# A hybrid diffusion backbone on one core: where the rounded half of a split operand is written

## The chip, the core and the metric

The kernel runs on one core of one Trainium2 chip. Its engines are TensorE (matrix products, into PSUM), VectorE (elementwise), ScalarE (copies and activation functions), GpSimd (elementwise, SBUF only) and SyncE, which here issues most of the DMAs. The metric is the device time of one execution in microseconds, the median of several runs.

## What is computed

Two layers over 1024 latent tokens of width 1024. Layer 0 mixes with pooling and differential attention, layer 1 with a gating MLP; each layer ends in an MLP with a squared ReLU. All data are float32. What matters here are three products of the same kind, each the second one of an MLP:

```python
def spatial_gating(h, w_in, ln_g, ln_b, sg_w, sg_b, w_out):
    ...
    return (u * mixed.reshape(b_, n, SG_WIDTH)) @ w_out      # (1024 x 2048) @ (2048 x 1024)

def sq_relu_ffn(h, w1, w2):
    return jnp.square(jax.nn.relu(h @ w1)) @ w2              # (1024 x 4096) @ (4096 x 1024)

for l in range(DEPTH):
    ...
    x = x + g1 * y                                           # l == 1: y = spatial_gating(...)
    x = x + g2 * sq_relu_ffn(modulate(...), ffn_w1[l], ffn_w2[l])
```

## The kernel before

Float32 accuracy is had from TensorE's rounded float32 type (F32R) by splitting each operand into a rounded half `hi` and the rest `lo` = x - hi. `split` (L101 to L104) does that with a ScalarE copy into `hi` (the write rounds) and a VectorE subtraction of `hi` from the source. `mm3` (L117 to L122) then makes three matmuls of each pair of operands: hi x hi (L120), hi x lo (L121), lo x hi (L122).

`ffn2` (L1239) is the second product of an MLP: layer 0's MLP, the gating MLP (weights `od_w_out`) and layer 1's MLP, in that order of time. The hidden values lie in DRAM (`hid_d`). Of the contraction, 512 rows at each end are done plainly (`accum`). What is between is done in blocks of 1024 rows: 3, 1 and 3 blocks. A block takes 7 products in place of 8 (Strassen's scheme in Winograd's form); each product has 4 token tiles of 128, and each tile 4 x 3 matmuls of 128x128 by 512 columns into one PSUM bank.

`block_prep` (L1122) is a generator that makes a block's operands. It loads the eight quarters of the block (`load`, L1127): four of hidden values (a11 to a22) and four of weights (b11 to b22), 1 MB each, and multiplies each weight quarter by the gate row on VectorE (L1137, both operands in SBUF). For each product `put` (L1152) splits the weights' operand in two halves of 128x1024 (`put_b`, L1140) and the hidden operand in four tiles of 128x512 (`put_a`, L1146). Between the products the quarters are added and subtracted in place, 128x2048 at a time, 8 a block, by GpSimd (L1169, L1172), but for two on VectorE in the first block of each second product (`E`, L1182). A quarter's buffer is loaded anew when its last reader is through.

`block` (L1209) runs the products. After each token tile VectorE adds the bank to U (L1229) or to the running result X (L1231); in a block's first product of a second product ScalarE copies it to U (L1227). Most banks are then accumulated on by the next product, so TensorE needs the add of that tile to be done before the next product's same tile. After each tile `step` takes one step of `block_prep`, four of which make the operands of one product. In layer 0's MLP every third step also makes one of 24 steps of layer 1's modulation (`ada_gen`, L141 to L169): 2 DMAs of 512 KB, 8 matmuls (L159) into a "tr" bank that is held over 8 such steps.

The order: TensorE and GpSimd keep the order of the program in `ffn2` (`pinned`, `pe_pool`). On the other engines and on SyncE's DMA queue a planner orders the instructions by its own costs, and each queue is then strictly in order. Buffers that hold work ahead: 8 tiles "hid" (one per token tile of a hidden operand, both halves), 10 tiles "w" (4 per weight operand), 8 tiles "h" for the quarters. PSUM has 8 banks: 5 "mm" for the products and 3 "tr" (`tr`, L92), used for transposes in other parts of the program and, in the blocks, by the modulation alone.

Of the kernel before, what the change touches and what calls it, by code (L numbers as in the profile page):

```python
# [10 lines left out]
F32R = mybir.dt.float32r  # L11
# [6 lines left out]
P = 128  # L18
# [12 lines left out]
SGW = 2048  # L31


# Issue order of the opening. The digit is a token tile (x, s, v, t, T, n), a block of 128 features
# (l, a, b, g, h, m), a pair of such blocks (w) or a piece of the rope tables (r).
# x/s/v/t/T/U: load, sum of squares, scale, transpose a token tile; l/a/b: load, multiply, turn the modulation into
# columns; g/h: modulate and split the first or second half of the tokens; w: weights of the first head;
# m/n: products of the first half by block or, for the last two blocks, by tile; q/r: rope tables; y: context tiles.
OPENING = (
# [7 lines left out]
class Net:  # L47
# [53 lines left out]
    def split(self, hi, lo, src):  # L101
        nc = self.nc
        nc.scalar.copy(out=hi, in_=src)  # L103
        nc.vector.tensor_sub(lo, src, hi.bitcast(F32))  # L104

    def load_split(self, src, shape, scale=None, mk=None):
        nc = self.nc
        mk = mk or self.w_tile
        raw = self.stage(shape)
        nc.sync.dma_start(out=raw, in_=src)  # L110
        if scale is not None:
            nc.vector.tensor_mul(raw, raw, scale)
        hi, lo = mk(shape), mk(shape)
        self.split(hi, lo, raw)
        return hi, lo
# [1006 lines left out]
    def block_prep(self, W, g2b, hp, n):  # L1122
        nc = self.nc
        G = nc.gpsimd
        raw, ahead = {}, {}

        def load(role, f0):  # L1127
            i, j = int(role[1]) - 1, int(role[2]) - 1
            t = self.big(self.h1 if role in ("b11", "a11", "b21", "a12") else self.h0, [P, 4, 512], F32)
            if role[0] == "a":  # L1130
                q = f0 // 256 + 2 * j
                for g in range(2):
                    nc.sync.dma_start(out=t[:, 2 * g:2 * g + 2], in_=self.hid_d[q + g, :, :, i * 512:(i + 1) * 512])
            else:
                s = slice(j * 512, (j + 1) * 512)
                nc.sync.dma_start(out=t, in_=W[f0 + i * 512:f0 + (i + 1) * 512, s].rearrange("(k p) n -> p k n", p=P))
                nc.vector.tensor_mul(t, t, g2b[:, s].unsqueeze(1).broadcast_to([P, 4, 512]))  # L1137
            ahead[role] = t

        def put_b(op, src, g, mk=None):  # L1140
            sh = [P, 2, 512]
            hi, lo = (mk or self.w_tile)(sh), (mk or self.w_tile)(sh)
            self.split(hi, lo, src[:, 2 * g:2 * g + 2])
            op[1].append((hi, lo))

        def put_a(op, src, ts):  # L1146
            for t in ts:
                z = hp.tile([P, 2, 4, P], F32R, tag="hid", name=self.name("hid"))
                self.split(z[:, 0], z[:, 1], src[:, :, t * P:(t + 1) * P])
                op[0].append(z)  # L1150

        def put(a, b, before=(), after=(), mk=None):  # L1152
            op = ([], [])
            self.ops.append(op)
            put_b(op, raw[b], 0, mk)
            yield
            put_b(op, raw[b], 1, mk)
            for f in before:
                f()
            yield  # L1160
            put_a(op, raw[a], (0, 1))
            yield
            put_a(op, raw[a], (2, 3))
            for f in after:
                f()
            yield

        def sub(o, x, y, eng=G):
            return lambda: eng.tensor_sub(raw[o], raw[x], raw[y])  # L1169

        def add(o, x, y, eng=G):
            return lambda: eng.tensor_add(raw[o], raw[x], raw[y])  # L1172

        for role in ("b11", "a11", "b21", "a12", "b22", "b12", "a21", "a22"):
            load(role, 512)
        for b in range(n):
            raw.update(ahead)
            f0 = 512 + (b + 1) * 1024
            more = b + 1 < n
            nx = lambda *roles: [lambda r=r: load(r, f0) for r in roles] if more else []  # L1180
            mk = None
            E = G if b else nc.vector  # L1182
            yield from put("a11", "b11", [sub("b12", "b22", "b12", E)], [sub("a11", "a11", "a21", E)])
            yield from put("a12", "b21", [add("b11", "b11", "b12"), sub("b21", "b21", "b11")])
            yield from put("a11", "b12", [sub("b12", "b22", "b11")], [add("a21", "a21", "a22")])
            yield from put("a22", "b21", nx("b11"), [sub("a22", "a22", "a11")] + nx("a11"))
            yield from put("a22", "b11", nx("b21"), [sub("a12", "a12", "a22")] + nx("b22"))
            yield from put("a21", "b12", nx("b12"), nx("a21"))
            if not more:
                halves = []  # L1190

                def mk(shape):
                    if not halves:
                        z = self.big(self.h1, [P, 4, 512])
                        halves.extend((z[:, 0:2], z[:, 2:4]))
                    return halves.pop(0)
            yield from put("a12", "b22", nx("a22"), nx("a12"), mk=mk)
# [255 lines left out]


class FfnPair:
    """One pair of feature tiles of the first product of an MLP: squared ReLU of it."""

    def __init__(self, net, i):
        self.net, self.i = net, i
# [17 lines left out]


class SgPair:
    """One group of the gating MLP: the gate times the values mixed along the tokens of a chunk."""  # L1480

    def __init__(self, net, i):
        self.net, self.i, self.v = net, i, {}
# [85 lines left out]
```

## Time and profile before

| | before |
|---|---|
| time, median of 3 runs | 2774.7 us (2770.87 to 2779.99) |
| span of the profiled execution | 2777.1 us |
| TensorE, matmul busy | 2612.3 us, 94% |
| VectorE busy | 1916.1 us, 69% |
| ScalarE busy | 1032.1 us, 37% |
| GpSimd busy | 993.7 us, 36% |

The page gives the span of the profiled execution, from its first to its last instruction, and no other time of it. In the rows PE is TensorE, DVE VectorE, ACT ScalarE, POOL GpSimd, SPq SyncE's DMA queue; L104 is line 104 of the kernel. An operation is written out<-in by the names of the program's tiles: `hid` is a split hidden tile, `w` a split half of weights, `h` a quarter, `ps` a product's bank, `x` the running result, `u` the tile U, `ad` the modulation's weights. A window has the stretch, its length, the busy time and number of instructions of PE, PEld (weight loads of TensorE), DVE, ACT and POOL, the granted TensorE clock as a share of full speed, the share of time that the DMA engines were busy, and GB/s. "[3.72 <-DVE x L1231]" says that the engine was idle for 3.72 us before, and that the DVE instruction of L1231 ended it. The end of a matmul is modelled, so its pace is read from the starts. A wait for several releasers is put down to the last.

### The profile page before, as it was taken

To read this page: it belongs to the slowest core of one execution; us is meant where nothing else is said; L and a number is where in the kernel's file an instruction comes from. 1 tells how busy PE (TensorE), PEld (TensorE's weight loads), DVE (VectorE), ACT (ScalarE), POOL (GpSimd) and SP (SyncE) were. 2 spreads that over 40 slices of the span, in tenths; PEclk is the share of its full clock that TensorE was granted. 3 is DMA by queue.
4 is the path that set the end of the run, shared out by engine and by line. 5 is a ranking of instruction groups with operands and counts; after the bars stand their busy time and mean duration, and the time that the engine had idled before them with its cause. 6 is when DMAs were issued, how large, how long until landed. Compare 5 with 4: busy or idle time off the path is not lost. (4 is left out here: it accounts for less than half of the span.)

```text
span 2777.1 us, 33164 instructions
## 1 busy us (share of the span) xinstructions
PE 2612.3 (94%) x12531; PEld 2128.2 (77%) x12531; DVE 1916.1 (69%) x2506; ACT 1032.1 (37%) x1827; POOL 993.7 (36%) x567
## 2 busy tenths in 40 slices
PE   6999989998999999979999999999899999988989
PEld 5888967777877888756677888887687888767767
DVE  5645678888486556698887624665978555689994
ACT  5322356666243333223334224542333333323330
POOL 5421357664053232144354202210545223043352
PEclk9999999999999999999999999999899999999999
DMA  8576532211233334544533323446032333622302
GB/s 259 169 220 212 194 112 97 91 63 41 97 110 103 121 107 135 211 166 171 205 106 133 117 93 110 136 152 238 24 122 77 121 106 121 241 92 91 121 8 91
DMA packets 202845, 360.15 MB, mean 130 GB/s; under 512 B 13231, under 2 KB 107266, under 8 KB 197566
## 3 DMA queue, kind: packets, MB, share of 16 engines
q1 hardware_dynamic: 183168, 290.01, 31.7%
q10 hardware_dynamic: 16158, 46.01, 4.5%
q0 software_dynamic: 3360, 22.02, 2.3%
q8 instruction: 99, 1.62, 0.2%
q14 instruction: 60, 0.49, 0.1%
HBM read 264.89 MB, written 93.10 MB: 129 GB/s over the span
## 5 line engine op out<-in xcount | busy, mean ns | idle before, releaser
L104 DVE TENSOR_TENSOR w<-s,w 128x512 fp32r<-128x512 f32 (+3 forms) x311 | 299.0, 976 | 208.8 <-ACT w L103 206.1
L120 PE MATMUL ps<-w,hid 128*128 128x512 f32 x928 | 378.6, 408 | 42.0 <-DVE x L1231 35.5
L122 PE MATMUL ps<-w,hid 128*128 128x512 f32 x928 | 371.7, 401 | 12.9 <-DVE hid L104 12.9
L121 PE MATMUL ps<-w,hid 128*128 128x512 f32 x928 | 371.6, 400 | 0.0
L103 ACT CAST w<-s 128x512 fp32r<-128x512 f32 (+2 forms) x313 | 212.6, 692 | 274.7 <-POOL s L1035 74.3
L1169 POOL TENSOR_TENSOR h<-h,h 128x2048 f32<-128x2048 f32 x36 | 176.1, 4892 | 256.5 <-DVE hid L104 91.9
L120 PEld LDWEIGHTS ps<-w,hid 128*128 128x128 f32 x928 | 180.7, 195 | 107.9 <-DVE x L1231 32.2
L103 ACT CAST hid<-h 128x512 fp32r<-128x512 f32 x196 | 116.6, 619 | 355.9 <-PE ps L122 184.6
L104 DVE TENSOR_TENSOR hid<-h,hid 128x512 fp32r<-128x512 f32 x196 | 234.9, 1213 | 8.8 <-ACT hid L103 8.7
L122 PEld LDWEIGHTS ps<-w,hid 128*128 128x128 f32 x928 | 180.6, 195 | 56.0 <-DVE hid L104 16.8
L121 PEld LDWEIGHTS ps<-w,hid 128*128 128x128 f32 x928 | 181.2, 195 | 36.8
L1035 POOL TENSOR_TENSOR s<-s,s 128x512 f32<-128x512 f32 x36 | 48.2, 1339 | 434.5 <-DVE w L104 434.3
L104 DVE TENSOR_TENSOR w<-h,w 128x1024 fp32r<-128x1024 f32 x92 | 184.8, 2013 | 2.3 <-ACT w L103 2.3
L1172 POOL TENSOR_TENSOR h<-h,h 128x2048 f32<-128x2048 f32 x14 | 77.2, 5513 | 272.3 <-DVE h L1169 185.7
L781 ACT ACTIVATE e<-sc,nm 128x1280 f32<-128x1280 f32 x96 | 127.5, 1328 | 108.3 <-DVE nm L775 106.6
L120 PE MATMUL ps<-h,w 128*128 128x512 f32 x416 | 164.0, 394 | 0.3 <-ACT h L205 0.3
L121 PE MATMUL ps<-h,w 128*128 128x512 f32 x416 | 162.3, 390 | 0.4 <-DVE h L206 0.4
L122 PE MATMUL ps<-h,w 128*128 128x512 f32 x416 | 162.6, 391 | 0.0
L765 PE MATMUL sc<-k,q 128*128 128x512 f32 (+1 forms) x576 | 139.1, 377 | 15.5 <-ACT e L781 14.0
L771 DVE TENSOR_REDUCE nm<-sc 128x1 f32<-128x768 f32 x192 | 148.5, 815 | 0.6 <-PE sc L765 0.6
L794 POOL TENSOR_TENSOR e<-e,e 128x1280 f32<-128x1280 f32 x47 | 136.4, 2902 | 3.9
L765 PEld LDWEIGHTS sc<-k,q 128*128 128x128 f32 x576 | 103.0, 192 | 42.2 <-ACT e L781 21.9
(313 smaller groups left out, 6405.7 us busy)
## 6 DMA issues: line engine op xcount, KB each, us to landing
ad<-in_ada_w_dram SPq DMA_DIRECT2D x96, 512.0 KB
s<-in_ffn_w_dram SPq DMA_DIRECT2D x80, 512.0 KB
hid_d<-h SPq DMA_DIRECT2D x28, 1024.0 KB
h<-hid_d SPq DMA_DIRECT2D x56, 512.0 KB
h<-in_ffn_w_dram SPq DMA_DIRECT2D x24, 1024.0 KB
s<-in_od_w_in_dram SPq DMA_DIRECT2D x32, 512.0 KB
k<-kt_d POOLq DMA_DIRECT2D x12, 1280.0 KB, 7.7
kt_d<-x SPq DMA_DIRECT2D x48, 256.0 KB
```

Source lines behind the costliest of these rows:

```text
L103: nc.scalar.copy(out=hi, in_=src)
L104: nc.vector.tensor_sub(lo, src, hi.bitcast(F32))
L120: nc.tensor.matmul(ps, ah, bh, start=first, stop=False, skip_group_check=more)
L121: nc.tensor.matmul(ps, ah, bl, start=False, stop=False, skip_group_check=more)
L122: nc.tensor.matmul(ps, al, bh, start=False, stop=last, skip_group_check=more)
L765: nc.tensor.matmul(s[:, o0:o0 + n], hd["q"][:, c, t * P:(t + 1) * P], hd["k"][:, c, a, o0:o0 + n], start=(a == 0), stop=(a == 1))
L771: self.nc.vector.tensor_reduce(st["nm"][c][:, i:i + 1], st["s"][c][:, s], axis=AX.X, op=ALU.max, negate=True)
L781: nc.scalar.activation(e, st["s"][c], AF.Exp, bias=nm[:, 0:1], accum_out=z)
L794: nc.gpsimd.tensor_add(e0, e0, e1)
L1035: G.tensor_add(a22, a21, a22)
L1169: return lambda: eng.tensor_sub(raw[o], raw[x], raw[y])
L1172: return lambda: eng.tensor_add(raw[o], raw[x], raw[y])
```

## The change

In `put_b` and `put_a`, and nowhere else, `split` is replaced by a new function `split_ps`. For each piece of 128x512 (a tile of `put_a` is one piece, a half of `put_b` two) ScalarE writes the rounded value to a "tr" PSUM bank as well, and VectorE subtracts that copy, not the one in SBUF. After the pieces, ScalarE writes the rounded half to SBUF, as before, for TensorE. So a tile of `put_a` takes two ScalarE copies of 128x512 and one subtraction; a half of `put_b` takes two copies of 128x512, two subtractions of 128x512 and a copy of 128x1024. The rest of the diff empties some comment lines.

```diff
+    def split_ps(self, hi, lo, src, parts):
+
+        nc = self.nc
+        for h, l, x in parts(hi, lo, src):
+            r = self.tr([P, 512]).rearrange("p (a n) -> p a n", a=x.shape[1])
+            nc.scalar.copy(out=r.bitcast(F32R), in_=x)
+            nc.vector.tensor_sub(l, x, r)
+        nc.scalar.copy(out=hi, in_=src)
...
         def put_b(op, src, g, mk=None):
             sh = [P, 2, 512]
             hi, lo = (mk or self.w_tile)(sh), (mk or self.w_tile)(sh)
-            self.split(hi, lo, src[:, 2 * g:2 * g + 2])
+            self.split_ps(hi, lo, src[:, 2 * g:2 * g + 2], lambda h, l, x: [(h[:, i:i + 1], l[:, i:i + 1], x[:, i:i + 1]) for i in range(2)])
             op[1].append((hi, lo))
 
         def put_a(op, src, ts):
             for t in ts:
                 z = hp.tile([P, 2, 4, P], F32R, tag="hid", name=self.name("hid"))
-                self.split(z[:, 0], z[:, 1], src[:, :, t * P:(t + 1) * P])
+                self.split_ps(z[:, 0], z[:, 1], src[:, :, t * P:(t + 1) * P], lambda h, l, x: [(h, l, x)])
                 op[0].append(z)
```

## Rows read from the trace of the kernel before

**Rows 1.** Windows of the three stretches; columns as in the profile section.

```profile
1160.20:1461.20 301.00, 274.49 (x1201) 195.12 (x1200) 267.15 (x222) 92.35 (x126) 132.19 (x37) 0.96 0.48 167
1934.80:2031.40 96.60, 83.59 (x338) 67.09 (x337) 88.29 (x69) 32.67 (x44) 54.59 (x18) 0.91 0.21 76
2448.00:2728.80 280.80, 246.92 (x1009) 198.53 (x1008) 267.31 (x219) 94.40 (x128) 133.84 (x34) 0.94 0.25 84
```

**Rows 2.** Order of time, TensorE: start us, us, line, operation; unstalled.

```profile
1261.65 0.39 PE L120 MATMUL ps<-w,hid 128*128 128x512 f32 x1
...
1266.41 0.39 PE L120 MATMUL ps<-w,hid 128*128 128x512 f32 x1
...
1267.18 1.06 PE L159 MATMUL tr<-ad,cstat 128*32 128x512 f32 x8
...
1268.51 0.39 PE L121 MATMUL ps<-w,hid 128*128 128x512 f32 x1
```

**Rows 3.** Order of time, TensorE, behind a stall in the last MLP.

```profile
2688.24 0.80 PE L120 MATMUL ps<-w,hid 128*128 128x512 f32 x1 [3.72 <-DVE x L1231]
...
2689.68 0.63 PE L120 MATMUL ps<-w,hid 128*128 128x512 f32 x1
...
2690.96 0.63 PE L120 MATMUL ps<-w,hid 128*128 128x512 f32 x1
```

**Rows 4.** Waits of TensorE, 1160 to 1456: us in total, times, longest us.

```profile
PE tr L159 <- DMA ad<-in_ada_w_dram: 18.5, 9, 6.3
```

**Rows 5.** Waits of TensorE, 2455 to 2712.

```profile
PE ps L120 <- DVE x L1231: 23.0, 9, 3.8
PE ps L120 <- DVE u L1229: 6.5, 2, 4.1
PE ps L122 <- DVE hid L104: 4.4, 3, 2.0
```

**Rows 6.** The page's costliest groups: busy us, mean ns | idle before, releaser.

```profile
L104 DVE TENSOR_TENSOR hid<-h,hid 128x512 fp32r<-128x512 f32 x196 | 234.9, 1213 | 8.8 <-ACT hid L103 8.7
...
L104 DVE TENSOR_TENSOR w<-h,w 128x1024 fp32r<-128x1024 f32 x92 | 184.8, 2013 | 2.3 <-ACT w L103 2.3
```

**Rows 7.** By line: count, duration ns min/median/max, first and last start.

```profile
L104 DVE TENSOR_TENSOR hid<-h,hid x196: 675/680/5114, 1142.9 to 2708.6; 128x512 fp32r<-128x512 f32 x196
L104 DVE TENSOR_TENSOR w<-h,w x92: 1208/1215/5641, 1128.8 to 2695.9; 128x1024 fp32r<-128x1024 f32 x92
...
L1231 DVE TENSOR_TENSOR x<-x,ps x140: 671/675/690, 1178.8 to 2729.1; 128x512 f32<-128x512 f32 x140
...
L1169 POOL TENSOR_TENSOR h<-h,h x36: 4496/4611/6552, 1177.9 to 2679.8; 128x2048 f32<-128x2048 f32 x36
```

**Rows 8.** Order of time, VectorE and GpSimd, start of the last MLP's blocks.

```profile
2471.72 5.67 DVE L104 TENSOR_TENSOR hid<-h,hid 128x512 fp32r<-128x512 f32 x2
2477.32 0.68 DVE L1231 TENSOR_TENSOR x<-x,ps 128x512 f32<-128x512 f32 x1
2477.91 5.05 DVE L104 TENSOR_TENSOR hid<-h,hid 128x512 fp32r<-128x512 f32 x2
...
2471.94 4.91 POOL L1169 TENSOR_TENSOR h<-h,h 128x2048 f32<-128x2048 f32 x1 [1.23 <-DVE w L104]
2476.79 5.02 POOL L1172 TENSOR_TENSOR h<-h,h 128x2048 f32<-128x2048 f32 x1
```

**Rows 9.** Order of time, ScalarE, same stretch.

```profile
2459.49 0.57 ACT L1227 COPY u<-ps 128x512 f32<-128x512 f32 x1
2459.96 1.05 ACT L103 CAST w<-h 128x1024 fp32r<-128x1024 f32 x1
2460.92 2.18 ACT L103 CAST hid<-h 128x512 fp32r<-128x512 f32 x4
```

**Rows 10.** Waits of VectorE, 2445 to 2715.

```profile
DVE h L1137 <- DMA h<-in_ffn_w_dram: 6.5, 9, 1.7
```

**Rows 11.** Waits of SyncE's DMA queue, 1150 to 1460.

```profile
SPq L1136 <- DVE w L104: 60.5, 6, 21.8
```

## The prediction

> **What bounds the kernel now.** I read the windows first, cut at the first and last block product of the three second products (layer 0's MLP, the gating MLP, layer 1's MLP; S1, S2, S3 below). They last 301.0, 96.6 and 280.8 us, 678.4 us of the span; VectorE is busy for 267.2, 88.3 and 267.3 us of them, and TensorE has idle time in each [rows 1]. The change touches nothing outside them but the first splits, just ahead. Next comes the pace that TensorE could keep. In an unstalled stretch 21 matmuls lie between two L120 rows, (1266.41 - 1261.65) / 21 = 0.2267 us each [rows 2]. A block is 7 products x 4 token tiles x 12 matmuls = 336, or 76.2 us. In S1 there are also 24 steps of the modulation: from L120 at 1266.41 to L121 at 1268.51 are 2.10 us, of which four paces are 0.91, so a step costs 1.19 us [rows 2], 28.6 us in all. The floors are then 228.5 + 28.6 = 257.1, 76.2 and 228.5 us, and the excess over them **43.9, 20.4 and 52.3 us: 116.6 us**. That is all this change can win.
>
> Who makes the excess: in S3, TensorE waits 23.0 + 6.5 us for bank adds of VectorE and 4.4 us for subtractions, 33.9 us in 14 waits [rows 5]. [...] In S1 another 18.5 us are waits for the modulation's weights [rows 4]; those DMAs stand on SyncE's queue behind block loads, which wait 60.5 us for VectorE's subtractions to give buffers back [rows 11].
>
> Why VectorE is late: the subtraction of a 128x512 piece takes 680 ns in the median and 5114 at worst, that of 128x1024 1215 and 5641 [rows 7]; the means are 1213 and 2013 [rows 6]. The order of time shows what stretches them: two subtractions take 5.67 us over a GpSimd sum that starts at 2471.94 and lasts 4.91, while the bank add at 2477.32, in the middle of the next GpSimd sum, takes 0.68 [rows 8]. The add has one operand in PSUM. All 140 of its kind lie between 671 and 690 ns, though GpSimd's sums of 4.5 to 6.6 us fill the same stretches [rows 7]. So an operation with both operands in SBUF waits until a running GpSimd sum is over, and one with an operand in PSUM doesn't.
>
> **The change, part by part.** *Removed:* 196 subtractions of 128x512 and 98 of 128x1024 lose their second SBUF operand. *In their place* come 196 + 2 x 98 = 392 of 128x512 with one operand in PSUM. Their nearest row is the bank add: 0.59 us from its start to the next one's (2477.32 to 2477.91) [rows 8] and 0.69 at most [rows 7]; I take 0.68. VectorE then saves 196 x (1.213 - 0.68) = 104 us and, on the 92 that the page groups, 92 x (2.013 - 1.36) = 60 us [rows 6], 164 us or 23.5 a block. In S3 its busy time falls from 267.3 to about 197 of 228.5 us; in S1 to about 197 of 257. It is no longer full, and what is left there is mostly paced by TensorE itself.
>
> [...]
>
> *Added:* 392 ScalarE copies of 128x512 from SBUF to PSUM. No row has a ScalarE write to PSUM. The nearest: a copy of that size out of PSUM is followed 0.47 us later by the next operation and lasts 0.57, and four casts SBUF to SBUF take 2.18 together, 0.55 each [rows 9]. Bounds 0.47 to 0.57; I take 0.55, the same source side. Per product ScalarE then has 8 x 0.55 + 4 x 0.55 + 2 x 0.96 (1024 columns: 2459.96 to 2460.92 [rows 9]) = 8.5 us of the product's 48 x 0.2267 = 10.9. I cost the copies at nothing: TensorE's products hide them, and buffers for about one product ahead stand between. Without that cover they would cost 392 x 0.55 = 216 us.
>
> *Moved:* the rounded half that TensorE reads is now written behind the PSUM copies, so it comes 0.55 us (one copy) or 1.1 us (two) later; the subtraction starts as before. No DMA moves. GpSimd's in-place sums wait for that last copy too, again about 1 us, against the 4 to 5 us that a held subtraction costs them now. *Added wait:* a PSUM copy needs one of the three "tr" banks, and the modulation holds one through S1. Queued behind a waiting copy are the rounded halves, the casts of the next operand and, in a block's first product, the copies into U; TensorE's next product and GpSimd's next sum wait for these. A bank is taken for 0.57 + 0.68 = 1.25 us; 8 a product on two banks are 5.0 us of 10.9. No cost.
>
> *What is late next:* the multiplications by the gate row (L1137) keep two SBUF operands, 4 a block, and stand in order on VectorE behind their loads, as yet with short waits: 9, longest 1.7 us, 6.5 in all in S3 [rows 10]. With VectorE early they can wait longer, or be held by GpSimd. I allow one TensorE wait per block of today's mean size, 33.9 / 14 = 2.42 us, with its tail 2.42 x 1.54 = 3.7 us; 7 blocks are 26.1 us. Of the modulation's 18.5 us I let half go, since the queue ahead of them moves earlier, and keep 9.2 for the transfers themselves.
>
> **Sum:** 116.6 - 26.1 - 9.2 = 81.3 us won. The profile gives 2777.1 us as the span of the profiled execution and no other time of it; that is 2.4 us above the median of the three runs (2774.7), so I take 2.4 off: 2777.1 - 81.3 - 2.4 = **2693 us**. If the whole excess goes, 2777.1 - 116.6 - 2.4 = 2658; that is the lower end.
>
> **Rivals.** *A, loads become the bound.* VectorE reaches each gate multiplication before its load has landed and stands, with the bank adds queued behind it. For: SyncE issues the loads only when buffers come back [rows 11], and VectorE waits at these lines even now [rows 10]. Against: those waits are short, and a bank add has the time of three tiles (36 matmuls, 8 us) before TensorE needs the bank. If every second of 28 costs TensorE a wait with tail, 14 x 3.7 = 52 us stay, with the 9.2 of the modulation 61; 55 us are won: 2720.
>
> *B, the change doesn't do what it says.* The new subtractions are held by GpSimd all the same, since their other operand is still in SBUF. Against: the 140 bank adds, built alike [rows 7]. Time: 2775.
>
> *C, slower: ScalarE becomes the bound.* The copy to PSUM is the one price that no row shows. ScalarE's old work is 4.1 us a product. It fills TensorE's 10.9 us once a copy costs (10.9 - 4.1) / 8 = 0.85 us. A product takes (678.4 - 28.6) / 49 = 13.3 us today, so the kernel gets slower from (13.3 - 4.1) / 8 = 1.15 us a copy, twice the nearest row. At 1.25 us: 14.1 us a product, 49 x 0.8 = 39 us lost: 2814. Against: reading PSUM is no dearer for it than reading SBUF [rows 9].
>
> **How the numbers follow.** Forecast (at most about one wait per block) 0.67, A 0.17, B 0.07, C 0.09. Faster by over 0.3%, which is about what a measurement of this kernel can tell from no change (8 us): the forecast and A, 0.84. Within 0.3%: B, 0.07. Slower: C, 0.09. The range starts at 2658, with nothing of the excess left, and goes past A to 2735, since A's number of waits is open: two waits a block and the whole 18.5 us kept leave 71 us, that is 2729. Outside stand B, C and the worst of A, about 2 in 10.
>
> **What would show it.** Right: no subtraction of these products above 0.7 us; VectorE below 90% in S3, TensorE's waits for VectorE there down from 33.9 us to under 12, its granted clock above 0.97; S3 near 240 us, S2 near 80, S1 near 278. A is right if VectorE's waits at L1137 grow to tens of us and TensorE waits for bank adds behind them. B: subtractions of 5 us remain. C: ScalarE near full in the stretches, VectorE and TensorE waiting for it, a copy to PSUM above 0.85 us. The forecast is wrong above all if the products are held by a chain that VectorE's lateness hides now, such as GpSimd's sums in order, 8 a block at 4.6 us in the median [rows 7]: 37 us of 76, free in total, but in series.

## The result and the profile after

| | before | changed |
|---|---|---|
| median of the runs | 2776.05 us (2770.87 to 2779.99) | 2670.71 us (2670.13 to 2671.41) |
| ratio, 95% interval | | 0.9615 [0.9598, 0.9632] |
| span of the profiled execution | 2777.1 us | 2669.6 us |
| S1, S2, S3 | 301.0, 96.6, 280.8 us | 267.5, 77.7, 229.8 us |
| the span outside them | 2098.7 us | 2094.6 us |

The changed kernel is 105.3 us faster. The forecast was 2693. Of the 107.5 us between the two spans, 103.4 lie in the three stretches and 4.1 outside. The lines of the code stand 9 lower down than before (8 in e3 and 10 in e6 below): the three matmuls are L129 to L131, the copy into PSUM is L111, its subtraction L112, the rounded half in SBUF L113, the gate multiplication L1146, GpSimd's sums L1178 and L1181, the bank add L1240.

The windows of the changed kernel, cut as [rows 1]:

```profile
1162.10:1429.60 267.50, 261.16 (x1201) 191.44 (x1200) 196.33 (x258) 169.06 (x280) 126.79 (x37) 1.00 0.55 189
1892.50:1970.20 77.70, 76.49 (x338) 63.02 (x337) 61.37 (x75) 51.18 (x84) 48.72 (x18) 1.00 0.25 86
2391.54:2621.38 229.84, 229.03 (x1009) 189.08 (x1008) 194.55 (x255) 169.23 (x281) 125.62 (x34) 1.00 0.30 103
```

In the last MLP VectorE's busy time fell from 267.31 to 194.55 us, ScalarE's rose from 94.40 to 169.23, and TensorE is busy for all but 0.8 us at a granted clock of 1.00 in place of 0.94. Above the floors of 257.1, 76.2 and 228.5 us are left 10.4, 1.5 and 1.3 us of what were 43.9, 20.4 and 52.3.

The subtractions that were held before are not held now. By line, with count and duration min/median/max, the new subtractions (answering to [rows 7]) and the two kinds of copies (the count at the end of a line is of a sample where it differs from the first):

```profile
L112 DVE TENSOR_TENSOR hid<-h,tr x196: 674/681/691, 1142.6 to 2601.6; 128x512 fp32r<-128x512 f32 x196
L112 DVE TENSOR_TENSOR w<-h,tr x184: 673/681/691, 1131.9 to 2588.0; 128x512 fp32r<-128x512 f32 x184
...
L113 ACT CAST hid<-h x196: 612/617/628, 1142.0 to 2599.9; 128x512 fp32r<-128x512 f32 x196
...
L1178 POOL TENSOR_TENSOR h<-h,h x36: 4601/4632/6557, 1179.5 to 2573.3; 128x2048 f32<-128x2048 f32 x36
...
L111 ACT CAST tr<-h x392: 571/580/595, 1126.0 to 2595.2; 128x512 fp32r<-128x512 f32 x196
```

No subtraction of the 380 lasts longer than 691 ns, and none of the 12 others longer than 692, while GpSimd's sums beside them are as long as ever; before, the longest were 5114 and 5641 [rows 7]. The gate multiplications, which keep two SBUF operands, are another matter (mean in ns; the time before them is waits for loads):

```profile
L1146 DVE TENSOR_TENSOR h<-h,row 128x2048 f32<-128x2048 f32 x28 | 76.5, 2733 | 48.4 <-DMA h<-in_ffn_w_dram 37.1 <-DMA h<-in_od_w_out_dram 11.3
```

Four of these 28 last 4.0 to 6.5 us where the others take 2.29; before, one did, 4.0 us.

The waits of TensorE in the last MLP, all of them (before: 33.9 us in 14 waits [rows 5]); then those in layer 0's MLP (before: 18.5 us for the modulation [rows 4] and 8.0 us for VectorE):

```profile
PE ps L129 <- DVE x L1240: 0.8, 2, 0.5
```

```profile
PE tr L168 <- DMA ad<-in_ada_w_dram: 3.9, 4, 1.7
PE ps L131 <- DVE hid L112: 2.4, 1, 2.4
```

The waits of VectorE in the last MLP (2391 to 2622), and the row of SyncE's queue in layer 0's MLP that answers to [rows 11]:

```profile
DVE hid L112 <- ACT tr L111: 21.8, 23, 3.6
DVE h L1146 <- DMA h<-in_ffn_w_dram: 3.3, 6, 1.3
...
DVE x L1240 <- PE ps L131: 2.8, 7, 0.9
```

```profile
SPq L1145 <- DVE w L112: 26.6, 6, 7.4
```

VectorE now waits for ScalarE, TensorE and loads, and has time for that. The queue's wait for the weights' subtractions has fallen from 60.5 to 26.6 us, and TensorE's wait for the modulation's weights from 18.5 to 3.9; how far the one made the other is taken up at e3.

### The profile page after: what moved, and what is told of

Its sections match the earlier page's. It is cut to its first block, busy times and chain, and to the rows that moved or that the text cites. A ratio compares the mean times of both kernels' runs of the same rounds, so it can differ in the third digit from the quotient of the medians.

```text
span 2669.6 us, 33659 instructions
## 1 busy us (share of the span) xinstructions
PE 2573.1 (96%) x12531; PEld 2112.1 (79%) x12531; DVE 1756.2 (66%) x2604; ACT 1229.0 (46%) x2219; POOL 975.4 (37%) x567
## 5 line engine op out<-in xcount | busy, mean ns | idle before, releaser
L129 PE MATMUL ps<-w,hid 128*128 128x512 f32 x928 | 365.6, 394 | 0.8 <-DVE x L1240 0.8
L131 PE MATMUL ps<-w,hid 128*128 128x512 f32 x928 | 361.7, 390 | 2.4 <-DVE hid L112 2.4
L130 PE MATMUL ps<-w,hid 128*128 128x512 f32 x928 | 361.6, 390 | 0.0
L111 ACT CAST tr<-h 128x512 fp32r<-128x512 f32 x392 | 220.5, 582 | 104.7 <-DVE w L112 49.3
L1178 POOL TENSOR_TENSOR h<-h,h 128x2048 f32<-128x2048 f32 x36 | 172.3, 4790 | 173.5 <-DVE h L1146 86.5
L129 PEld LDWEIGHTS ps<-w,hid 128*128 128x128 f32 x928 | 174.5, 188 | 56.9 <-issue 9.3
L131 PEld LDWEIGHTS ps<-w,hid 128*128 128x128 f32 x928 | 174.5, 188 | 39.5 <-DVE hid L112 2.8
L130 PEld LDWEIGHTS ps<-w,hid 128*128 128x128 f32 x928 | 174.6, 188 | 35.1
L1181 POOL TENSOR_TENSOR h<-h,h 128x2048 f32<-128x2048 f32 x14 | 70.6, 5042 | 266.8 <-DVE h L1178 266.8
L129 PE MATMUL ps<-h,w 128*128 128x512 f32 x416 | 164.5, 396 | 0.3 <-ACT h L214 0.3
L131 PE MATMUL ps<-h,w 128*128 128x512 f32 x416 | 162.8, 391 | 0.0
L112 DVE TENSOR_TENSOR hid<-h,tr 128x512 fp32r<-128x512 f32 x196 | 130.3, 683 | 46.8 <-ACT tr L111 43.9
L774 PEld LDWEIGHTS sc<-k,q 128*128 128x128 f32 x576 | 103.4, 193 | 41.2 <-ACT e L790 20.7
L113 ACT CAST hid<-h 128x512 fp32r<-128x512 f32 x196 | 118.4, 617 | 36.7 <-PE ps L130 21.8
```

The costliest lines, as they stand in the source:

```text
L111: nc.scalar.copy(out=r.bitcast(F32R), in_=x)
L112: nc.vector.tensor_sub(l, x, r)
L129: nc.tensor.matmul(ps, ah, bh, start=first, stop=False, skip_group_check=more)
L130: nc.tensor.matmul(ps, ah, bl, start=False, stop=False, skip_group_check=more)
L131: nc.tensor.matmul(ps, al, bh, start=False, stop=last, skip_group_check=more)
L774: nc.tensor.matmul(s[:, o0:o0 + n], hd["q"][:, c, t * P:(t + 1) * P], hd["k"][:, c, a, o0:o0 + n], start=(a == 0), stop=(a == 1))
```

## The experiments

**The theories.** *H*, the theory of the prediction: a subtraction with both operands in SBUF is held until a running GpSimd sum ends; in its narrow form, only GpSimd's reading of SBUF does that. *L*, a rival: VectorE simply has too much to do, and whatever takes time from it gives the gain. *O*, another rival (P in the expectations): the gain is that of another order, since the planner lays out VectorE's, ScalarE's and SyncE's instructions anew when 392 copies are added. Stretches are given as S1/S2/S3, and what lies outside them as the rest; medians are compared with the kernel before on the same chip.

**One half of the change alone.** e1_hidden keeps the change for the hidden operand only, e2_weights for the weights' only.

```diff
 # e1_hidden, from the changed kernel, in put_b
-            self.split_ps(hi, lo, src[:, 2 * g:2 * g + 2], ...)
+            self.split(hi, lo, src[:, 2 * g:2 * g + 2])
 # e2_weights, from the changed kernel, in put_a
-                self.split_ps(z[:, 0], z[:, 1], src[:, :, t * P:(t + 1) * P], ...)
+                self.split(z[:, 0], z[:, 1], src[:, :, t * P:(t + 1) * P])
```

> Only the hidden operand's tiles (put_a) go by way of PSUM; the weights' halves are split as before. Theory H (VectorE's subtractions with two SBUF operands were held by GpSimd's sums, and that made TensorE wait): of the 164 us of holding, 104 go and 60 stay, so something over half of the 105 us is won: 2695 to 2720 us; no subtraction of the hidden tiles above 0.7 us, those of the weights' halves still up to 5 us. Rival P (the planner's new order, not the holding, made the gain): no relation to these shares; time anywhere between 2670 and 2776, with subtractions of the weights no longer than in the kernel before but TensorE's waits gone or unchanged alike.

> Only the weights' halves (put_b) go by way of PSUM; the hidden tiles are split as before. H: 60 of 164 us of holding go: 2720 to 2750 us, and the hidden tiles' subtractions are still held up to 5 us. If the two gains (this and the hidden tiles alone) add up to clearly more than 105 us, either alone already takes VectorE off the bound; if to clearly less, both had to go. P: as for the hidden tiles alone.

Measured: e1 2727.0 us, ratio 0.9827 [0.9806, 0.9849], stretches 279.5/86.9/269.2; e2 2732.3 us, 0.9854 [0.9837, 0.9872], 276.9/91.3/272.7. The subtractions that each left as they were, on the page's costliest groups (busy us, mean ns | idle before), e1's and e2's:

```profile
L104 DVE TENSOR_TENSOR w<-h,w 128x1024 fp32r<-128x1024 f32 x92 | 200.0, 2178 | 29.3 <-ACT w L103 29.3
```

```profile
L104 DVE TENSOR_TENSOR hid<-h,hid 128x512 fp32r<-128x512 f32 x196 | 265.8, 1372 | 41.9 <-ACT hid L103 41.3
```

Both means rose, from 2013 to 2178 and from 1213 to 1372 [rows 6], and with the unheld durations that e5 gives below, 88 us of holding are left in e1 where the weights' subtractions had 73, and 134 in e2 where the hidden ones had 103. It looks as if a sum that no longer meets the one kind of subtraction meets the next of the other kind, so that the holding is in part handed on; in e3, where the order is new too but nothing is cured, the means do not rise (1977 and 1169). e1 missed its expectation by 7 us: that had reckoned with 60 us of holding left. e2 lies inside its range. In the stretches the halves win 42.8 and 37.6 us, 80.4 together, and the whole change 103.4; in S3 they win 11.6 and 8.1, and the whole 51.0. Both kinds had to go.

**The copies without their use.** e3_unread writes the PSUM copies but subtracts the half in SBUF, as before.

```diff
 # from the changed kernel, in split_ps
             nc.scalar.copy(out=r.bitcast(F32R), in_=x)
-            nc.vector.tensor_sub(l, x, r)
-        nc.scalar.copy(out=hi, in_=src)
+        self.split(hi, lo, src)
```

> ScalarE writes the PSUM copies as in the changed kernel, but nothing reads them: the subtraction takes the SBUF half as before. H: no gain, since the subtractions still have two SBUF operands; 2770 to 2795 us, the upper part if ScalarE's 392 extra copies (8.5 us of 10.9 a product) reach the path; subtractions up to 5 us remain. P: if the extra instructions win by changing the order, below 2740.

Measured: 2758.9 us, 0.9949 [0.9931, 0.9966], 288.1/92.4/285.7, rest 2086.3. The subtractions still last up to 5107 and 5644 ns. Neither expectation was met: the time lies between H's 2770 to 2795 us and the 2740 of the rival. That the median fell by 14 us with all the holding left speaks for O in part. In the profiled executions S1 is 13.0 us shorter, S2 4.2 shorter, S3 4.9 longer, the rest 12.4 shorter. The order alone is thus worth some ten us either way in a stretch. It does not carry the change: S2 and S3 together are 0.7 us longer in e3 and 69.9 shorter in the changed kernel. ScalarE was busy for 168.0 of S3's 285.7 us, and the added copies cost the kernel no time here. Against e3, which has the same added copies, the changed kernel is 88 us faster.

Most of what e3 wins in S1 lies in TensorE's wait for the modulation's weights, 18.5 us before. In e3, with the subtractions held as before, it is:

```profile
PE tr L167 <- DMA ad<-in_ada_w_dram: 7.4, 3, 2.7
```

So of the 14.6 us by which this wait is shorter in the changed kernel, e3 has 11.1 without any cure.

**The sums on VectorE.** e4_vecsums is the kernel before with GpSimd's sums moved to VectorE, more work on the engine that L holds to be overloaded.

```diff
-            return lambda: eng.tensor_sub(raw[o], raw[x], raw[y])
+            return lambda: nc.vector.tensor_sub(raw[o], raw[x], raw[y])
...
-            return lambda: eng.tensor_add(raw[o], raw[x], raw[y])
+            return lambda: nc.vector.tensor_add(raw[o], raw[x], raw[y])
```

> The kernel before, with GpSimd's in-place sums of the quarters put on VectorE instead (8 a block of about 2.29 us each, as the two there take already). VectorE gets more work, but nothing holds it. H: subtractions at 0.68 and 1.21 us throughout; VectorE's work is then 194.6 / 3 (its busy time per block in the changed kernel) + 18 = about 80 us a block against 76 for TensorE, so it bounds by a little: 7 x 4 to 7 x 8 us over the changed kernel, 2695 to 2730 us. Rival L (VectorE was simply overloaded, and less work is what helped): its 267 us of 281 in the last MLP grow by 3 x 18 less what was there, so slower than before, 2850 us or more.

Measured: 2682.8 us, 0.9675 [0.9659, 0.9691], 260.5/79.7/235.3. By line, its subtractions, and the window of its last MLP:

```profile
L104 DVE TENSOR_TENSOR hid<-h,hid x196: 676/687/1789, 1143.8 to 2613.9; 128x512 fp32r<-128x512 f32 x196
L104 DVE TENSOR_TENSOR w<-h,w x92: 1216/1221/1231, 1129.9 to 2600.6; 128x1024 fp32r<-128x1024 f32 x92
```

```profile
2396.45:2631.76 235.31, 229.95 (x1010) 188.73 (x1008) 229.01 (x236) 91.11 (x126) 23.08 (x12) 1.00 0.28 96
```

The only subtractions that are still held, eight of the hidden ones at 1.77 to 1.79 us, all start beside one of the sums of 1.7 to 2.2 us that GpSimd keeps at the end of S2 and S3 (128x512, X plus U). VectorE is busy for 229.0 of 235.3 us here, 97%. Before it was 267.3 of 280.8 us [rows 1], but much of that was holding: in e5 below, with nothing held, the same instructions take 185.5. So VectorE has some 44 us more to do here than they need, and yet the stretch is 45 us shorter. L falls: not the amount of work was the trouble, but the held subtractions, with the bank adds behind them. The time is below the expected 2695 to 2730 us, since VectorE's work is 76 us a block and not 80. The three stretches sum to 575.5 us, as in the changed kernel (575.0); the 12 us between the two medians lie outside them.

**GpSimd that writes and does not read.** e5_writeonly is the kernel before with two fills in place of each GpSimd sum; the sums are left out of the computation.

```diff
+            def put_in():
+                if eng is not G:
+                    return eng.tensor_sub(raw[o], raw[x], raw[y])
+                for _ in range(2):
+                    G.memset(raw[o], 1.0)
```

> The kernel before, splits untouched, with each of GpSimd's in-place sums of the quarters replaced by two memsets of the same target: GpSimd stays busy at the same places and writes SBUF, but reads nothing (the sums are left out of the computation). H in its narrow form (it is GpSimd's reading that a second SBUF operand of VectorE waits for): subtractions at 0.68 and 1.21 us although both operands lie in SBUF, products near their floor, 2665 to 2690 us. Rival W (any GpSimd work that uses SBUF holds VectorE): subtractions up to the length of a memset pair longer, 2720 us or more.

Measured: 2659.3 us, 0.9592 [0.9575, 0.9610]. The subtractions by line, the costliest kind of fill (mean 1813 ns), and the three windows:

```profile
L104 DVE TENSOR_TENSOR hid<-h,hid x196: 679/687/695, 1142.7 to 2587.7; 128x512 fp32r<-128x512 f32 x196
L104 DVE TENSOR_TENSOR w<-h,w x92: 1217/1220/1227, 1128.2 to 2574.9; 128x1024 fp32r<-128x1024 f32 x92
```

```profile
L1173 POOL MEMSET h<- 128x2048 f32 x72 | 130.2, 1813 | 305.1 <-DVE w L104 124.9 <-DVE h L1137 91.0 <-DVE hid L104 87.2
```

```profile
1159.60:1417.60 258.00, 258.00 (x1201) 191.19 (x1200) 191.08 (x223) 95.05 (x127) 95.88 (x54) 1.00 0.57 197
1886.90:1963.10 76.20, 76.20 (x337) 63.08 (x337) 63.27 (x70) 33.40 (x44) 37.19 (x20) 1.00 0.27 96
2379.40:2607.90 228.50, 228.50 (x1010) 189.21 (x1009) 185.48 (x219) 95.35 (x128) 93.87 (x52) 1.00 0.30 104
```

GpSimd works for 94 of S3's 228.5 us and no subtraction is held, so rival W of the expectation falls; the time is even below the 2665 us expected. All three stretches last as long as the floors of the prediction (257.1, 76.2, 228.5), S1 0.9 us longer. It also gives the unheld durations, 687 and 1221 ns, and with them the holding before: 196 x (1.213 - 0.687) + 92 x (2.013 - 1.221) = 176 us [rows 6].

**GpSimd that reads one operand.** e11_readone is the same with two scalings, each with one source of 128x2048 in SBUF (and one column, `eps`); again the sums are left out.

```diff
-                    G.memset(raw[o], 1.0)
+                    G.tensor_scalar(raw[o], raw[x], self.eps, 1.0, op0=ALU.mult, op1=ALU.mult)
```

> As with the memsets, but each of GpSimd's sums of the quarters is replaced by two scalings out of one other quarter (one SBUF source, one target; the sums are left out of the computation). Narrow H (a second SBUF operand of VectorE waits while GpSimd reads): subtractions are held again, up to the 2 to 4 us that one or both scalings last, and the time goes back most of the way: 2700 to 2760 us. If it takes GpSimd's two sources to hold VectorE: subtractions at 0.69 and 1.22 us, 2655 to 2675.

Measured: 2686.2 us, 0.9702 [0.9682, 0.9722], 270.0/81.0/239.1. Its subtractions by line, and the scalings (mean 2652 ns):

```profile
L104 DVE TENSOR_TENSOR hid<-h,hid x196: 675/686/2396, 1141.6 to 2615.9; 128x512 fp32r<-128x512 f32 x196
L104 DVE TENSOR_TENSOR w<-h,w x92: 1210/1220/2943, 1125.1 to 2605.0; 128x1024 fp32r<-128x1024 f32 x92
```

```profile
L1173 POOL TENSOR_SCALAR h<-h,eps 128x2048 f32<-128x2048 f32 x72 | 190.8, 2652 | 256.8 <-DVE w L104 90.2 <-DVE h L1137 87.5 <-DVE hid L104 75.8
```

They are held again, up to 1.7 us. So H is right in its narrow form: it is what GpSimd reads, and one full-sized source is enough. Beside fills, which only write, the longest subtraction of a hidden tile is 695 ns (e5), beside these scalings 2396 (e11).

The time was below what we expected (2700 to 2760). The means are 1025 and 1579 ns, so 196 x 0.338 + 92 x 0.358 = 99 us are held here, and the stretches stand only 28 us above their floors; in e1 it was 92 x (2.178 - 1.221) = 88 us held, and 74 above. The pieces differ: at most 1.7 us in e11, up to 5646 - 1223 = 4423 ns in e1. This would fit a short hold being mostly taken up by the lead that VectorE has on TensorE, and a long one not. It is argued from these two runs and not shown; no run varied the length alone.

**ScalarE's price doubled.** e6_double writes each PSUM copy twice.

```diff
+            for _ in range(2):
+                nc.scalar.copy(out=r.bitcast(F32R), in_=x)
-            nc.scalar.copy(out=r.bitcast(F32R), in_=x)
```

> The changed kernel with every ScalarE copy to PSUM made twice. A copy follows the last one by 0.52 us in the changed kernel's trace, so ScalarE goes from 8 x 0.52 + 4 x 0.52 + 2 x 0.96 = 8.2 us a product to 12.3, over TensorE's 10.9. If ScalarE is as near to being the bound as the prediction reckoned (full at 0.85 us a copy): 49 x 1.4 = about 70 us over the changed kernel, 2725 to 2750 us, with ScalarE near full in the stretches. If the lead of the splits hides it: below 2685.

Measured: 2749.3 us, 0.9914 [0.9899, 0.9929], 297.6/79.9/264.6. The window of its last MLP, and TensorE's longest wait there:

```profile
2428.04:2692.55 264.51, 241.52 (x1010) 191.21 (x1008) 180.80 (x250) 243.47 (x430) 118.75 (x34) 0.97 0.25 83
```

```profile
PE ps L132 <- DVE hid L113: 19.5, 15, 5.4
```

ScalarE is busy for 243.5 of 264.5 us, and S3 takes 264.5 / 21 = 12.6 us a product. That is what rival C feared, ScalarE as the bound, made on purpose and at the upper end of the expected 2725 to 2750 us. At 2 x 0.52 = 1.04 us a piece the kernel is still faster than before, as rival C's own arithmetic has it: slower only from 1.15 us. In the changed kernel ScalarE has 169.2 of 229.8 us.

**A smaller ring.** A "tr" bank is taken from the copy to the end of the subtraction. To see what fewer banks cost, two of the three were to be held through each second product (one in layer 0's MLP, where the modulation holds another). In e7_onebank the planner let them go again early:

```diff
+        held = [self.tr([P, 512]) for _ in range(1 if nxt == self.next_l1 else 2)]
+        for z in held:
+            nc.vector.memset(z, 0.0)
...
+        for z in held:
+            nc.vector.tensor_copy(out=self.small([P, 1], "ss"), in_=z[:, 0:1])
```

> The changed kernel with only one of the three tr banks left for the splits in the blocks (two are held by tiles written once before and read once after; in layer 0's MLP one, beside the modulation's). A bank is taken for a copy, 0.58 us, and a subtraction, 0.68, and some hand-over: 8 a product are 10 to 12 us against TensorE's 10.9. If the ring is what the prediction reckoned: just at the bound, 2675 to 2730 us. If ScalarE's copies had to run well ahead of VectorE (the ring matters more than its arithmetic): over 2750. If the hand-over costs nothing: 2671.

Measured: 2665.6 us, 0.9611 [0.9595, 0.9627], 267.9/77.9/229.8, rest 2088.4. ScalarE's order of time has three PSUM copies in a row, so the ring was whole and nothing follows on it. Its ratio is not told apart from the changed kernel's 0.9615; the stretches are as long, and what lies outside them is 6 us shorter in the profiled execution, though e7 takes no work away there. The three copies in a row:

```profile
2429.55 1.62 ACT L111 CAST tr<-h 128x512 fp32r<-128x512 f32 x3
```

e9_onebank holds them to the end, since their reader adds the (zero) banks to the last tile of the running result:

```diff
-            nc.vector.tensor_copy(out=self.small([P, 1], "ss"), in_=z[:, 0:1])
+            nc.vector.tensor_add(X[3][:, 512:1024], X[3][:, 512:1024], z)
```

> Repeats the one-bank run with held tiles that last: their readers are now adds (of zeros) onto the result behind the last block product, since in the earlier run the trace shows three ScalarE copies to PSUM in a row, so its held tiles had been let go early and the ring was whole. One tr bank for the splits in all three stretches. A copy (0.58) and a subtraction (0.68) with hand-over then take turns: 8 a product are 10 to 12 us against TensorE's 10.9. Prediction's ring: 2675 to 2730 us, the more since other work stands between on both queues. If the planner arranges the order around it at no cost: 2660 to 2672.

Measured: 2741.4 us, 0.9895 [0.9876, 0.9913], 289.3/83.7/276.8. ScalarE's waits in the last MLP (2440 to 2700), its order of time there, and TensorE's longest wait:

```profile
ACT tr L111 <- DVE w L112: 35.5, 38, 2.2
ACT tr L111 <- DVE hid L112: 35.3, 69, 3.3
```

```profile
2461.18 0.59 ACT L111 CAST tr<-h 128x512 fp32r<-128x512 f32 x1 [0.20 <-DVE hid L112]
2461.71 0.61 ACT L113 CAST hid<-h 128x512 fp32r<-128x512 f32 x1
2462.53 0.59 ACT L111 CAST tr<-h 128x512 fp32r<-128x512 f32 x1 [0.20 <-DVE hid L112]
```

```profile
PE ps L131 <- DVE hid L112: 31.2, 17, 4.7
```

One bank costs 71 us, and 75 in the stretches, more than we expected (2675 to 2730 us). Copy and subtraction take turns, 2462.53 - 2461.18 = 1.35 us a piece, as the prediction's 1.25; 8 pieces are then 10.8 us of a product's 10.9, with no room for anything else. In the changed kernel the same waits of ScalarE come to 13.5 + 11.0 us in S3 with three banks and 7.7 + 14.7 in S1 with two, and TensorE's waits behind them to 0 and 2.4 us.

**A faster version.** In the first products of the MLPs the token sums (`sums`) are still split in the old way, beside GpSimd sums, and a ScalarE copy for which TensorE waits (L1081: 9.5 us in 3 waits over the whole span) stands behind them. Two of the changed kernel's rows there, VectorE in order of time, 128x1024 that takes 1.21 us unheld, and the wait of TensorE:

```profile
2070.34 2.83 DVE L104 TENSOR_TENSOR T<-T,T 128x1024 fp32r<-128x1024 f32 x1 [0.52 <-ACT T L103]
...
2073.21 3.29 DVE L104 TENSOR_TENSOR x<-x,x 128x1024 fp32r<-128x1024 f32 x1
...
2079.30 0.80 PE L129 MATMUL ps<-T,w 128*128 128x512 f32 x1 [4.34 <-ACT t L1081]
```

e8_sums gives these sums the new split too; e10_two_on_vec moves two of a block's GpSimd sums to VectorE on top of that.

```diff
 # e8_sums, from the changed kernel, in sums, three times
-            self.split(T1[0][:, s], T1[1][:, s], t)
+            self.split_ps(T1[0][:, s], T1[1][:, s], t, ...)
 # e10_two_on_vec, on top of it
-            yield from put("a22", "b21", nx("b11"), [sub("a22", "a22", "a11")] + nx("a11"))
-            yield from put("a22", "b11", nx("b21"), [sub("a12", "a12", "a22")] + nx("b22"))
+            yield from put("a22", "b21", nx("b11"), [sub("a22", "a22", "a11", nc.vector)] + nx("a11"))
+            yield from put("a22", "b11", nx("b21"), [sub("a12", "a12", "a22", nc.vector)] + nx("b22"))
```

> The changed kernel, and the splits of the token sums ahead of the first products (three places, 128x1024 each, held up to 3.4 us by GpSimd too) by way of PSUM as well. TensorE waits there for 1.6 + 4.3 us (copies of the first product) and a few more for subtractions. If the holding makes these: 4 to 8 us off, 2663 to 2667 us. If something else in that stretch is late (the sums themselves): 2671.

> The kernel with the token sums' splits by way of PSUM too, and in the blocks the sums that free the last two hidden quarters (a22 - a11, a12 - a22) on VectorE (2.29 us) in place of GpSimd (4.6). If layer 0's MLP is left 10 us over its floor because block loads, and behind them the modulation's, wait for these sums: that stretch falls from 267 to about 261 us and the time from 2651.6 to 2643 to 2648. If VectorE's two-operand sums, held by GpSimd's others, cost as much as they save: 2649 to 2656.

Measured: e8 2651.6 us (2650.5 to 2652.7), 0.9561 [0.9547, 0.9576], 267.3/78.0/229.9, rest 2075.7; e10 2646.2 us (2639.2 to 2650.7), 0.9548 [0.9527, 0.9570], 263.5/76.2/229.2, rest 2077.8. e8 is 19 us faster than the changed kernel by the medians (15 by the ratios, each against the kernel before on its own chip), all of it outside the stretches, and faster than either expectation. The rest lies between 2085.9 and 2104.9 us in the kernels with the old splits there, so about 10 us lie beyond that spread; how the other 9 divide is not settled. Of the waits at L1081, two (4.3 and 3.6 us) are gone in e8 and one of 1.6 is left. e10's interval overlaps e8's, though its S1 is 3.8 us shorter (263.5 us where about 261 was expected); the step between the two times is not told apart with certainty. In e10's S1 TensorE no longer waits for the modulation's weights, and no gate multiplication is held (the longest takes 2295 ns).

## Why the prediction was right, and where it was off

The direction and the mechanism were right, and the time came out 23 us below the forecast, inside the range and nearer to its lower end, where the whole excess is gone. By its own steps:

- **Why VectorE was late.** Right, and shown: e5 and e11 take the reading away and give half of it back, e4 takes the sums away, and in the changed kernel not one of the new subtractions is held. Rival B falls with the same row.
- **The new subtraction, 0.68 us.** Measured 0.681. VectorE's busy time in S1 and S3 was to fall to 197 us; it fell to 196.3 and 194.6. A PSUM operand does not make the subtraction dearer here: 681 ns with one, 687 unheld without (e5).
- **The copy into PSUM, 0.55 us, at no cost.** A copy lasts 0.58 and the next operation starts 0.52 us later. ScalarE was reckoned at 8.5 of 10.9 us a product, 78%; it is busy for 169.2 of 229.8 in S3, 74%. e6 bears out the arithmetic of rival C: with a second copy ScalarE fills the product, at 12.6 us where that arithmetic gives 4.1 + 16 x 0.52 = 12.4.
- **The ring, no cost.** Right for the kernel as it is, and not by a wide margin: ScalarE does wait for a bank, 24.5 us in S3, which the 5.0 of 10.9 us did not lead to expect, but TensorE does not wait behind it. With one bank it costs 71 us (e9).
- **What is late next: one TensorE wait of 3.7 us per block, 26.1 us in all.** This is the term that was mis-sized. In S2 and S3, four blocks, 2.8 us stand above the floors where 4 x 3.7 = 15 were left; in S1 10.4 where 3 x 3.7 + 9.2 = 20 were. No run shows the factor 1.54 in the 3.7 as a property of a wait: it is S3's excess by its waits before, 52.3 / 33.9, and the same quotient is 1.28 in e4 (6.8 / 5.3), 1.42 in e1 (40.7 / 28.7) and 1.69 in e11 (10.6 / 6.3). That matmuls are slower for a time behind a wait is in the trace: behind the stall of 3.72 us they stand 0.427 us apart [rows 3], at a granted clock of 0.50 from 2688.24 to 2691.50, and 0.2267 us apart [rows 2] at 1.00 from 1261.65 to 1266.41. The gate multiplications do have to wait for their loads, as expected, but 3.3 us in S3 with 1.3 the longest, less than before (6.5 and 1.7 [rows 10]); rival A did not come about. What did come, and was named as possible, is that GpSimd holds some of them: four of 28, 12 us in all where 2 were. TensorE's waits for bank adds in S3 are still only 0.8 us, so this cost next to nothing.
- **The modulation's 18.5 us, half of it kept.** 3.9 us are left. The reason that was given, the queue behind held subtractions, is shown only in part: in e3, with the subtractions held as before, these waits were 7.4 us already. Another order alone can thus take most of them away, and how much the holding had to do with it stays open.
- **The sum.** 35.3 us were kept of the excess and 13.2 remained: 22.1 us. The rest of the span fell by 4.1 us, and the median now lies 1.1 us above the profiled span where 2.4 below was carried over, which takes back 3.5. Together that is the 22.7 us between 2693.4 and 2670.7. The sum has no term for a new order of the other engines; e3 moved the time by 14 us through order alone, so a part of the 22.7 us, and of the gain, may be that and not the mechanism.

What was to be seen came: no subtraction above 0.7 us, VectorE at 85% in S3, TensorE's waits there at 0.8 us, the clock at 1.00, and S1, S2 and S3 at 267.5, 77.7 and 229.8 where 278, 80 and 240 were named.

Still open: how much of S1's 33.5 us and of the 4 us outside is the planner's order, since e3 had 13.0 and 12.4 us there without any cure. The 10.4 us left in S1 come apart as follows: 6.3 are TensorE's waits, 3.2 its longer busy time (261.16 us against 258.00 in e5, which has no waits), and 0.9 were never to be had, since e5 stands at 258.0 where the prediction's floor was 257.1.

## What to carry to other kernels

Look at the spread of a VectorE instruction's duration, not only its mean: where operations with two SBUF operands range from their usual time up to that of a GpSimd instruction beside them, they are being held (here 0.68 to 5.1 us beside sums of 4.5 to 6.6 [rows 7]), and everything queued behind them on VectorE with them (here bank adds, for which TensorE waited 29.5 us in S3 [rows 5]). Give one operand from PSUM, if ScalarE has the time for a copy (here 74% busy afterwards) and banks are free for a ring (with two, in S1, TensorE waited 2.4 us behind it; with one the time rose by 71 us, e9); do it for all such operations of the stretch at once, since the hold in part passes to those that are left (42.8 and 37.6 us for the halves, 103.4 for both). Sums moved from GpSimd to VectorE won as much in the stretches here (575.5 us against 575.0), with a VectorE that is then 97% full in the last MLP and without a copy on ScalarE. When variants of such a program are compared, split the difference by stretch first: an order that changes without any cure moved the time by 14 us (e3).

## What the runs showed of the hardware

- The holding goes both ways: in the changed kernel a GpSimd sum that starts beside VectorE's two-operand sums takes 6.49 us, the next one 4.63. The 1.86 us between them are about what VectorE's pair still had to run, 2404.26 - 2402.29 = 1.97. VectorE's and GpSimd's rows in order of time:

```profile
2399.77 4.49 DVE L1178 TENSOR_TENSOR h<-h,h 128x2048 f32<-128x2048 f32 x2
```

```profile
2402.29 6.49 POOL L1181 TENSOR_TENSOR h<-h,h 128x2048 f32<-128x2048 f32 x1 [87.00 <-DVE h L1178]
2408.86 4.63 POOL L1178 TENSOR_TENSOR h<-h,h 128x2048 f32<-128x2048 f32 x1
```

- ScalarE's write of 128x512 into PSUM lasts 580 ns in the median, into SBUF 617, but in a row the two are worth the same, about 0.52 us from one start to the next:

```profile
2407.10 0.61 ACT L113 CAST hid<-h 128x512 fp32r<-128x512 f32 x1
2407.61 0.58 ACT L111 CAST tr<-h 128x512 fp32r<-128x512 f32 x1
2408.13 0.62 ACT L113 CAST hid<-h 128x512 fp32r<-128x512 f32 x1
2408.66 0.58 ACT L111 CAST tr<-h 128x512 fp32r<-128x512 f32 x1
```

- 99 us of holding in pieces of at most 1.7 us cost some 28 us (e11), 88 us in pieces of up to 4.4 us some 74 (e1).
